# Modulation steps called from the output projection, the second GEMM's first operands loaded ahead of the residual, and stacked keys and queries turned by fp32r products

## The chip, the cores and the metric

The kernel runs on one core of a Trainium2 chip. The metric is the device time of one execution in microseconds (us); lower is better. Several executions of the kernel before were timed, and one more was profiled; the rows in this document come from the profiled one.

## The reference

Two transformer blocks work one after the other on one sequence of 1024 tokens of width 1024, all in float32. The first block projects the normalised tokens and runs three attentions on them: a sliding-window one, a sparse one that keeps the 256 best keys of each token by an index score, and one over 256 memory rows. Their outputs are projected, gated and summed, and the output projection adds the result to the residual:

```python
x = x + jnp.einsum("bsd,de->bse", merged, w_out[l])
h = rmsnorm(x, g_mlp[l])
hid = jnp.square(jax.nn.relu(jnp.einsum("bsd,df->bsf", h, w_mlp_in[l])))
x = x + jnp.einsum("bsf,fd->bsd", hid, w_mlp_out[l])
```

The second block mixes tokens by a gated recurrent scan in two directions and by pooling, and has an MLP of the same sizes (1024 to 4096 to 1024). Its norms are shifted and scaled by a modulation vector, which depends on a conditioning vector `c` alone and on nothing of the sequence:

```python
c_act = jax.nn.silu(c)
mod = c_act @ w_ada[l] + b_ada[l]          # 1024 -> 6144
sh1, sc1, gt1, sh2, sc2, gt2 = jnp.split(mod, 6, axis=-1)
```

## The kernel before, in words

Every large matrix product is made of three fp32r products: each operand is split into a rounded high part and a low remainder, and high times high, high times low and low times high are summed in PSUM. For a weight tile, ScalarE writes the high part (`wh`) and VectorE or GpSimd the low part (`wl`), in `wunit` and `parts_of`.

The order of work on each engine and each DMA queue is fixed when the program is built: a planner walks the program, gives each instruction a start by its own costs, and takes what is ready and stands earliest in the program. So an instruction may be issued well ahead of its place in the source, as soon as its data and its memory are free, but each engine and queue runs its own list strictly in order. A tile waits only for the last users of the memory that it takes over.

The stages that matter here, in order of time:

- *Attention.* `stack_q` and `stack_k` put the high and low parts of a 128-token tile of queries or keys side by side; `turn_q` and `turn_k` turn these stacks by TensorE transposes against `ident` (lines 349 and 371), four per tile of queries and two per head of keys. Between them, `fill` puts gate products (`gates_ahead`, lines 267 to 269) whose tiles stand in the pool `fwp`, the first above the weight pool on the right side of SBUF.
- *Gated sum.* For each of eight column tiles the sparse attention's projection and gate are added and split (lines 974 to 977).
- *Output projection*, `out_proj`: two halves of the tokens, eight steps of 24 products each. Before each step it calls `pre` (for the first block `x_cols`, which transposes a 128-column slice of the residual); after it, `upd` adds the product to the residual and `Stat.add` sums squares. When a half is done, its statistics give the row scale (`Stat.cols`, `spread`), and `post_out` builds the MLP's operand: `make_h` for the first half of the tokens, `make_t` for the second.
- *MLP*, `mlp`, called once for each block. Each of its two GEMMs is cut into 2 by 2 blocks with seven instead of eight block products (sums and differences of operands). The first GEMM has 16 steps `m`; the sums of weight tiles (`sums`, lines 1284 to 1287) are GpSimd's, the outputs q12, t1, t2, q21, t3, q22 and t4 are stored to DRAM (`ml_...`). The second GEMM takes four chunks `ch`; `second` loads one stored operand and splits it (ScalarE the high part, VectorE and GpSimd the low part, lines 1370 and 1371), `quarter` loads a quarter of weights, GpSimd makes sums and differences of the quarters (lines 1432, 1450, 1451, 1454), and `upd` adds each product into the residual, which is loaded back from DRAM (line 1356) into the tiles that held the first GEMM's intermediate results.
- *Modulation*, `ada`: a generator with 12 groups of 512 columns. Each group takes eight loads of 256 KB of `w_ada` into a ring of two tiles `adaw` (line 1197, SP's DMA queue), and for each load one VectorE step (line 1199 for the first, 1201 for the others). Then four TensorE transposes (line 1207) and a VectorE reduction give four columns of `mod`. `tick` advances it by one load. Before, the first block's MLP calls it: four times in each step `m` of the first GEMM and three times at each `tick2` of the second. Its pool `modp` stands where the output projection's operands (`m_hi`, `m_lo`) were.

All loads named so far go through SP's queue, most stores through ScalarE's. `begin` in `mlp` holds the pieces of the last statistics and of `make_t` that are left from the projection; `rest_t` is its second half.

Of the kernel before, what the change touches and what calls it, by code (L numbers as in the profile page):

```python
# [19 lines left out]
P = 128  # L20
# [40 lines left out]
def block_kernel(ctx, tc, x, mem, positions, g_mix, w_in, b_gate, sinks, g_mem, w_mem_kv, w_proj_swa, w_proj_dsa,  # L61
# [25 lines left out]
    def raw(ap):  # L87
        return ap.bitcast(F32)
# [23 lines left out]
    def tp_bank():  # L112
        return bank("tp")
# [5 lines left out]

    ident = cst([P, P], tag="ident")  # L120
    make_identity(nc, ident)
    mhalf = cst([P, 1], tag="mhalf")
    V.memset(mhalf, -0.5)

# [20 lines left out]
    def col(name, i):  # L145
        r0, _ = ROWS[name]
        return cols[:, r0 + i:r0 + i + 1]
# [6 lines left out]
    def h_tiles(pool):  # L154
        return tuple(pool([P, DC, 512], F32R, tag=f"h_{n}") for n in ("hi", "lo"))
# [188 lines left out]
    def turn_q(pool, st, nh):  # L344

        fill(nf["q"])
        pt = tp_bank()
        for h in range(nh):
            T.transpose(pt[:, h * P:(h + 1) * P], raw(st[:, h]).rearrange("p a b -> p (a b)"), ident)
        qT = pool([P, nh, P], F32R, tag=f"qT{nh}", bufs=QTB)  # L350
        A.copy(qT, pt[:, :nh * P].rearrange("p (h q) -> p h q", h=nh))
        return qT
# [12 lines left out]
    def turn_k(sts, dst):  # L365

        for h, st in enumerate(sts):
            fill(nf["k"])
            pt = tp_bank()
            for z in range(2):  # L370
                T.transpose(pt[:, z * P:(z + 1) * P], raw(st[:, 2 * z:2 * z + 2, :]).rearrange("p a b -> p (a b)"),
                            ident)
            for z, d in enumerate(dst(h)):
                A.copy(d, pt[:, z * P:(z + 1) * P])

# [714 lines left out]
    def mlp_dram(pool):  # L1090
        d = {n: pool([P, NM, 512], tag=f"ml_{n}") for n in OUTS}
        d["x"] = pool([P, DC, S], tag="ml_x")
        return d
# [50 lines left out]
                split_to(t4[0][:, c, :], t4[1][:, c, :], b[c])  # L1144
        rest_t.append(rest)

    xT = [hB([P, DC, 512], tag=n) for n in ("h_hi", "h_lo")]
    stp = Pool("stp", side="right", n512=4)
    xtp = Pool("xtp", side="right")
    HT[:] = [h_tiles(hA), None]  # L1150
    xs = {}

    def x_cols(hf, e):

        if e == 0:
            for j in range(4):
                xs[j] = xtp([P, D], tag="xt", bufs=4)
                nc.scalar.dma_start(xs[j], x[0, (4 * hf + j) * P:(4 * hf + j + 1) * P, :])
        pt = tp_bank()
        for j in range(4):  # L1160
            T.transpose(pt[:, j * P:(j + 1) * P], xs[j][:, e * P:(e + 1) * P], ident)
        A.copy(xT[hf][:, e, :], pt)

    mlp_d = mlp_dram(drm)

    def post_out(hf, rs):
        src = xT[hf]
        (make_h if hf == 0 else make_t)(stp, HT[hf], lambda c: src[:, c, :], rs, lambda c: col("g_mlp", c))

    pend = out_proj(stp, w_out[0], lambda k, hf: (m_hi[k][:, halves(hf)], m_lo[k][:, halves(hf)]),  # L1170
                    with_x_out(mlp_d, add_to(xT)),
                    post_out, x_cols)
    xtp.close()
    mgp.close()
    hBp = Pool("hBp")
    HT[1] = h_tiles(hBp)


    mod = cst([P, 48], tag="mod")
    bada = cst([P, 48], tag="bada")  # L1180
# [1 line left out]
    def ada(modp):  # L1182
        badr = modp([48, P], tag="badr")
        nc.scalar.dma_start(badr, b_ada_2[0].rearrange("(k p) -> k p", p=P))
        pt = tp_bank()
        T.transpose(pt[:, :48], badr, ident[:48, :48])
        V.tensor_copy(bada, pt[:, :48])
        r0, _ = ROWS["c_2"]
        s_ = modp([P, 64], tag="silu")[:, :DC]
        A.activation(s_, cols[:, r0:r0 + 8], AF.Tanh, scale=0.5)  # L1190
        V.scalar_tensor_tensor(s_, s_, 1.0, cols[:, r0:r0 + 8], op0=OP.add, op1=OP.mult)
        V.tensor_scalar(s_, s_, 0.5, None, op0=OP.mult)
        for g in range(12):
            acc = modp([P, 512], tag="ada", bufs=1)
            for k in range(DC):
                w = modp([P, 512], tag="adaw", bufs=2)
                nc.sync.dma_start(w, w_ada_2[0, k * P:(k + 1) * P, halves(g)])
                if k == 0:
                    V.tensor_scalar(acc, w, s_[:, 0:1], None, op0=OP.mult)
                else:  # L1200
                    V.scalar_tensor_tensor(acc, w, s_[:, k:k + 1], acc, op0=OP.mult, op1=OP.add)
                yield
            yield
            m4 = mod[:, g * 4:(g + 1) * 4]
            pt = tp_bank()
            for j in range(4):
                T.transpose(pt[:, j * P:(j + 1) * P], acc[:, j * P:(j + 1) * P], ident)
            V.tensor_reduce(m4, pt.rearrange("p (j q) -> p j q", j=4), axis=AX.X, op=OP.add)
            V.tensor_tensor(m4, m4, bada[:, g * 4:(g + 1) * 4], op=OP.add)

    def mlp(PB, xt, d, w1, w2, scale, post, begin, middle, tick=lambda: None, gains=None, each=lambda i, e: None,
            parts=((0, 0, 512), (1, 0, 512))):
# [75 lines left out]

        first_two(0, w_of(wp, 0, "wr", 2))
        begin[0]()  # L1290
        first_two(1, w_of(wp, 2, "wr", 2), begin[1])
        first_two(2, w_of(wp, 4, "wr", 2), eng=G)
        rest_t.pop()()
        begin[2]()
# [3 lines left out]
        for m in range(NM):  # L1298
# [10 lines left out]
            product(a, half(ua, 1), TQ["t2"])  # L1309
            V.tensor_tensor(u2, a, u2, op=OP.add)  # L1310
            V.tensor_tensor(q12, p5, u2, op=OP.add)
            for _ in range(2):
                tick()
            ub = parts_of(e1s.pop(m))
            a = mm_bank()
            product(a, half(ub, 1), B22)
# [11 lines left out]
            V.tensor_tensor(q22, p5, u3, op=OP.add)  # L1328
            relu2(q22)
            save("q22", m, q22)  # L1330
            for _ in range(2):
                tick()
            a = mm_bank()
            product(a, u4, TQ["t4"])
            V.tensor_tensor(u3, a, u3, op=OP.add)
# [15 lines left out]
        tick()  # L1351


        for hf, es in ((1, range(4)), (0, range(8)), (1, range(4, 8))):
            for e in es:
                nc.sync.dma_start(xt[hf][:, e, :], d["x"][:, e, halves(hf)])
        braw = hA([P, DC, 512], F32, tag="h_lo")
        nb = [0]

# [20 lines left out]
            return t_  # L1380

        def tick2():
            for _ in range(3):
                tick()

        def gather(to, a, ch):
# [38 lines left out]
        for ch in range(4):  # L1425
# [5 lines left out]
            for c in (0, 2):  # L1431
                G.tensor_tensor(s_[:, c:c + 2], a21[:, c:c + 2], a22[:, c:c + 2], op=OP.add)  # L1432
            b = second("q12", ch)
            for e, wt in blocks(a11):
                a = mm_bank()
                product(a, wt, b)
                gather(U[e], a, ch)
                upd(1, e, a)
            a12 = quarter(ch, 1, 0)
            tick2()  # L1440
            b = second("t1", ch)
            for e, wt in blocks(s_):
                a = mm_bank()
                product(a, wt, b)
# [87 lines left out]

    def post_mlp1(hf, st):
        if hf == 0:
            for _ in ada_["it"]:
                pass
            for i, n in ((0, "g_mix_2"), (1, "g_ffn_2")):
                r0, _ = ROWS[n]
# [21 lines left out]
               lambda c: mod[:, c:c + 1])  # L1560
        yield

    ada_ = {}

    def begin1():
        stp.close()
        ada_["it"] = ada(pools["mod"])

    def middle1():
        pools["stm"] = Pool("stm", side="right", n512=2)  # L1570

    def tick1():
        next(ada_["it"], None)

    pools["mod"] = Pool("modp")
    mlp(hBp, xT, mlp_d, w_mlp_in[0], w_mlp_out[0], None, post_mlp1,
        (lambda: next(pend), lambda: next(pend), begin1), middle1, tick1, gsq)
    pools["mod"].close()
    drm.close()
    HT[:] = h2  # L1580

# [107 lines left out]
            gates_half(0)  # L1689
    gates_half(1)  # L1690
    pools["stm"].close()
    pt = tp_bank()
    for t in range(NT):
        T.transpose(pt[:, t * 16:(t + 1) * 16], zT[:, t * P:(t + 1) * P], ident[:16, :16])
# [403 lines left out]
```

## Time and profile before

| | |
|---|---|
| median of 3 runs | 2720.86 us (2717.14 to 2721.62) |
| the profiled execution | 2721.95 us, of which the span from first to last instruction is 2720.2 us |
| mean granted TensorE clock | 0.972 of full speed |
| busy share of the span | PE (matmul) 93%, PEld (weight loads) 77%, DVE (VectorE) 69%, ACT (ScalarE) 44%, POOL (GpSimd) 36% |
| DMA | 338.57 MB, 124 GB/s over the span |
| first block's output projection | about 781 to 880 us |
| first block's MLP, first GEMM's 16 steps | about 943 to 1300 us |
| second block's MLP, first GEMM's 16 steps | about 2091 to 2378 us |

Reading it: times are us from the span's start unless marked ns. A busy PE is not yet PE at its peak: at the lower of the two clocks each matmul takes longer and counts as busy all the same. "A <- B" in a row of waits means that A's engine sat idle until B was done; the numbers after it are the us in total, how many times, and the longest. `SPq`, `ACTq` are DMA queues' own instructions. The engine names are those of the table.

### The profile page before, as it was taken

How to read it: one execution, taken by the hardware profiler on the slowest of the kernel's cores; microseconds unless marked ns; L12 is line 12 of the kernel's file. 1: busy time of each engine (PE TensorE's matmuls, PEld its weight loads, DVE VectorE, ACT ScalarE, POOL GpSimd, SP SyncE). 2: the span in 40 equal slices, each digit the busy share in tenths (PEclk: the TensorE clock that was granted, in tenths of full speed). 3: DMA queues.
4: the chain of work that ended last, by engine and by line, in shares of the span. 5: the costliest groups of instructions: out<-in, count | busy, mean ns of one | idle time of the engine just before them, and what ended most of it. 6: DMA issues, size and time to landing. Idle time of an engine off the chain costs nothing. (4 is left out here: it accounts for less than half of the span.)

```text
span 2720.2 us, 34915 instructions
## 1 busy us (share of the span) xinstructions
PE 2528.9 (93%) x12560; PEld 2107.4 (77%) x12560; DVE 1882.7 (69%) x3206; ACT 1197.9 (44%) x2218; POOL 988.1 (36%) x717
## 2 busy tenths in 40 slices
PE   7999999899999678888899979999997999989997
PEld 6899987788878566667688856888786788768886
DVE  7685878834455866676778896755658565578898
ACT  6575765335334433334433333323335554543433
POOL 3011123421002533333755661211334443476554
PEclk9999999999999889999999989999998999999999
DMA  3121022321155266666644301422343444753431
GB/s 114 53 61 40 25 79 90 89 61 41 63 183 179 78 203 200 202 204 230 220 170 155 109 24 51 156 63 70 120 152 97 160 150 159 250 204 134 170 109 62
DMA packets 275712, 338.57 MB, mean 124 GB/s; under 512 B 14268, under 2 KB 185044, under 8 KB 268372
## 3 DMA queue, kind: packets, MB, share of 16 engines
q1 hardware_dynamic: 234820, 253.65, 29.2%
q10 hardware_dynamic: 40720, 82.70, 8.3%
q8 instruction: 99, 1.62, 0.2%
q14 instruction: 73, 0.60, 0.1%
HBM read 250.25 MB, written 86.05 MB: 124 GB/s over the span
## 5 line engine op out<-in xcount | busy, mean ns | idle before, releaser
L1233 PE MATMUL mm<-h_hi,wh 128*128 128x512 f32 (+1 forms) x1136 | 455.5, 401 | 33.3 <-ACT wh L1227 17.2
L1235 PE MATMUL mm<-h_hi,wl 128*128 128x512 f32 (+1 forms) x1136 | 452.1, 398 | 10.5 <-DVE wl L1228 10.5
L1234 PE MATMUL mm<-h_lo,wh 128*128 128x512 f32 (+1 forms) x816 | 322.2, 395 | 0.0
L1233 PEld LDWEIGHTS mm<-h_hi,wh 128*128 128x128 f32 x1136 | 221.4, 195 | 82.2 <-ACT wh L1227 20.6
L1235 PEld LDWEIGHTS mm<-h_hi,wl 128*128 128x128 f32 x1136 | 220.7, 194 | 63.4 <-DVE wl L1228 18.2
L1227 ACT CAST wh<-q 128x1024 fp32r<-128x1024 f32 x116 | 121.7, 1052 | 331.7 <-PE mm L1234 297.7
L1234 PE MATMUL mm<-h_hi,wh 128*128 128x512 f32 (+1 forms) x624 | 244.8, 392 | 13.2 <-POOL h_hi L1371 13.2
L1228 DVE TENSOR_TENSOR wl<-q,wh 128x1024 fp32r<-128x1024 f32 x116 | 162.9, 1405 | 32.9 <-ACT wh L1227 31.3
L1234 PEld LDWEIGHTS mm<-h_lo,wh 128*128 128x128 f32 x816 | 158.3, 194 | 31.6
L1371 POOL TENSOR_TENSOR h_hi<-h_lo,h_hi 128x512 fp32r<-128x512 f32 x76 | 128.6, 1712 | 113.1 <-ACT h_hi L1370 107.9
L133 ACT CAST wh<-wr 128x1024 fp32r<-128x1024 f32 (+5 forms) x107 | 97.2, 911 | 149.7 <-PE mm L418 43.5
L1233 PE MATMUL mm<-q,wh 128*128 128x512 f32 x384 | 151.3, 394 | 10.4 <-DVE q L1119 10.4
L1235 PE MATMUL mm<-q,wl 128*128 128x512 f32 x384 | 150.2, 392 | 8.0 <-DVE wl L1228 8.0
L1234 PE MATMUL mm<-q,wh 128*128 128x512 f32 x384 | 150.9, 393 | 0.0
L1234 PEld LDWEIGHTS mm<-h_hi,wh 128*128 128x128 f32 x624 | 120.5, 193 | 37.9 <-POOL h_hi L1371 14.4
L1284 POOL TENSOR_TENSOR sa<-wr 128x512 f32<-128x512 f32 x32 | 41.7, 1303 | 264.8 <-DMA wr<-in_w_ff_dram 60.5
L134 POOL TENSOR_TENSOR wl<-wr,wh 128x1024 fp32r<-128x1024 f32 (+5 forms) x40 | 78.1, 1958 | 160.7 <-ACT wh L133 159.2
L1615 PE MATMUL mm<-h_hi,wh 128*128 128x512 f32 x320 | 132.0, 412 | 0.8 <-DVE kn L1648 0.8
L1617 PE MATMUL mm<-h_hi,wl 128*128 128x512 f32 x320 | 126.7, 396 | 0.0
L1371 DVE TENSOR_TENSOR h_hi<-h_lo,h_hi 128x512 fp32r<-128x512 f32 x76 | 120.4, 1605 | 8.3 <-ACT h_hi L1370 8.3
L1616 PE MATMUL mm<-h_lo,wh 128*128 128x512 f32 x320 | 125.5, 392 | 0.0
L1233 PE MATMUL mm<-h_lo,wh 128*128 128x512 f32 (+1 forms) x304 | 115.4, 380 | 0.6 <-ACT wh L1227 0.6
(589 smaller groups left out, 7006.9 us busy)
## 6 DMA issues: line engine op xcount, KB each, us to landing
h_lo<-ml_t SPq DMA_DIRECT2D x32, 1024.0 KB
adaw<-in_w_ada_dram SPq DMA_DIRECT2D x96, 256.0 KB
h_lo<-ml_q SPq DMA_DIRECT2D x24, 1024.0 KB
wr<-in_w_in_dram SPq DMA_DIRECT2D x42, 512.0 KB
wr<-in_w_out_dram SPq DMA_DIRECT2D x32, 512.0 KB
ml_t<-h_lo ACTq DMA_DIRECT2D x64, 256.0 KB
q<-in_w_mlp_out_dram SPq DMA_DIRECT2D x16, 1024.0 KB
ml_t<-x ACTq DMA_DIRECT2D x64, 256.0 KB
```

The source lines that it names most:

```text
L133: A.copy(hi, r)
L134: (eng or V).tensor_tensor(lo, r, raw(hi), op=OP.subtract)
L1227: A.copy(hi, r)
L1228: (eng or V).tensor_tensor(lo, r, raw(hi), op=OP.subtract)
L1233: mm(a, wt[0][:, k], b[0][:, k, sl], start=(k == 0), stop=False)
L1234: mm(a, wt[0][:, k], b[1][:, k, sl], start=False, stop=False)
L1235: mm(a, wt[1][:, k], b[0][:, k, sl], start=False, stop=(k == 3))
L1284: G.tensor_tensor(sa[:, 0:4], e2[:, 0:4], e2[:, 4:8], op=OP.add)
L1371: (G if c % 2 else V).tensor_tensor(lo[:, c], r[:, c], raw(hi[:, c]), op=OP.subtract)
L1615: mm(a, hi[:, k, :], r_hi, start=(k == 0), stop=False)
L1616: mm(a, hi[:, k, :], r_lo, start=False, stop=False)
L1617: mm(a, lo[:, k, :], r_hi, start=False, stop=(k == DC - 1))
```

## The change

```diff
+    identR = cst([P, P], F32R, tag="identR")
+    V.tensor_copy(identR, ident)
...
     # turn_q
-            T.transpose(pt[:, h * P:(h + 1) * P], raw(st[:, h]).rearrange("p a b -> p (a b)"), ident)
+            mm(pt[:, h * P:(h + 1) * P], st[:, h].rearrange("p a b -> p (a b)"), identR, start=True, stop=True)
     # turn_k
-                T.transpose(pt[:, z * P:(z + 1) * P], raw(st[:, 2 * z:2 * z + 2, :]).rearrange("p a b -> p (a b)"),
-                            ident)
+                mm(pt[:, z * P:(z + 1) * P], st[:, 2 * z:2 * z + 2, :].rearrange("p a b -> p (a b)"), identR,
+                   start=True, stop=True)
...
     # ada (now defined ahead of the output projection)
-                nc.sync.dma_start(w, w_ada_2[0, k * P:(k + 1) * P, halves(g)])
+                nc.gpsimd.dma_start(w, w_ada_2[0, k * P:(k + 1) * P, halves(g)])
...
-            yield
+            for _ in range(3):
+                yield
             m4 = mod[:, g * 4:(g + 1) * 4]
...
+    modp = Pool("modp", side="right")
+    ada_ = ada(modp)
+    def tick1(n=1):
+        for _ in range(n):
+            next(ada_, None)
...
     # x_cols
         A.copy(xT[hf][:, e, :], pt)
+        tick1(4)
...
     # mlp, ahead of the first GEMM's steps
-        first_two(1, w_of(wp, 2, "wr", 2), begin[1])
+        first_two(1, w_of(wp, 2, "wr", 2))
+        begin[1]()
...
     # mlp, first GEMM, at both places of step m
-            for _ in range(2):
-                tick()
+            tick()
...
     # mlp, second GEMM
-        for hf, es in ((1, range(4)), (0, range(8)), (1, range(4, 8))):
-            for e in es:
-                nc.sync.dma_start(xt[hf][:, e, :], d["x"][:, e, halves(hf)])
+        def x_back():
+            for hf, e0 in ((0, 0), (0, 4), (1, 0), (1, 4)):
+                nc.sync.dma_start(xt[hf][:, e0:e0 + 4, :], d["x"][:, e0:e0 + 4, halves(hf)])
...
         def tick2():
-            for _ in range(3):
+            for _ in range(2):
                 tick()
...
             b = second("q12", ch)
+            if not ch:
+                bt = second("t1", ch)
+                x_back()
             for e, wt in blocks(a11):
                 a = mm_bank()
                 product(a, wt, b)
                 gather(U[e], a, ch)
-                upd(1, e, a)
+                upd(1, e, a if ch else U[e])
             a12 = quarter(ch, 1, 0)
             tick2()
-            b = second("t1", ch)
+            b = second("t1", ch) if ch else bt
...
-    pools["mod"] = Pool("modp")
     mlp(hBp, xT, mlp_d, w_mlp_in[0], w_mlp_out[0], None, post_mlp1,
         (lambda: next(pend), lambda: next(pend), begin1), middle1, tick1, gsq)
-    pools["mod"].close()
...
     # second block, after its gates
     pools["stm"].close()
+    modp.close()
```

So the modulation's generator starts ahead of the output projection, in a pool on the right side of SBUF that stays open until the second block's gates; its loads are issued by GpSimd; four of its steps stand in each of the 16 projection steps, two in each step `m`, two at each `tick2`, and three instead of one step lie between a group's last load and its transposes. The changes in `mlp` hold for both blocks; only the first block passes it a `tick`.

## Rows read from the trace of the kernel before

**Rows 1.** The page's part 1: busy us (share of the span) xinstructions of each engine.

```profile
PE 2528.9 (93%) x12560; PEld 2107.4 (77%) x12560; DVE 1882.7 (69%) x3206; ACT 1197.9 (44%) x2218; POOL 988.1 (36%) x717
```

**Rows 2.** Windows: stretch, length, PE, PEld, DVE, ACT, POOL busy (xcount), PEclk, DMA share, GB/s.

```profile
716.00:781.00 65.00, 65.00 (x286) 53.37 (x287) 30.75 (x51) 20.83 (x33) 0.00 (x0) 1.00 0.45 140
781.00:880.00 99.00, 97.49 (x461) 79.09 (x460) 50.49 (x61) 39.60 (x59) 17.35 (x13) 1.00 0.58 184
880.00:943.00 63.00, 41.00 (x163) 32.02 (x162) 54.08 (x69) 26.94 (x45) 30.95 (x20) 0.81 0.27 84
943.00:1300.00 357.00, 305.26 (x1260) 240.64 (x1259) 245.69 (x316) 141.49 (x213) 129.21 (x91) 0.94 0.63 209
...
2091.00:2378.00 287.00, 281.41 (x1230) 231.37 (x1229) 160.73 (x199) 145.55 (x213) 125.69 (x91) 0.99 0.53 177
```

**Rows 3.** The tile adaw: op xcount, ns min/median/max, first and last start; who waited.

```profile
L1197 SPq DMA_DIRECT2D adaw<-in_w_ada_dram x96: 327/328/1405, 880.0 to 1227.2; - x96
L1201 DVE SCALAR_TENSOR_TENSOR ada<-adaw,silu,ada x84: 732/752/1803, 888.0 to 1232.2; 128x512 f32<-128x512 f32 x84
L1199 DVE TENSOR_SCALAR ada<-adaw,silu x12: 473/600/1469, 886.5 to 1214.4; 128x512 f32<-128x512 f32 x12
...
  DVE ada L1201: 61.4, 36
```

**Rows 4.** Waits of SP's queue, 945 to 1300 us: us, times, longest.

```profile
SPq L1197 <- DVE ada L1201: 65.4, 73, 2.6
SPq L1197 <- DMA adaw<-in_w_ada_dram: 52.4, 34, 4.0
SPq L1197 <- DVE ada L1199: 39.2, 8, 6.2
```

**Rows 5.** Waits of PE: whole span, and 880 to 945 us.

```profile
PE tp L1207 <- DVE ada L1201: 26.4, 9, 12.2
...
PE tp L1035 <- POOL st_r L127: 10.2, 1, 10.2
```

**Rows 6.** Line 267, the gate filler's products: first and last start.

```profile
L267 PE MATMUL fl<-h_hi,fh x160: 387/396/628, 101.8 to 714.2; 128*128 128x512 f32 x160
```

**Rows 7.** DMA issues between 945 and 1300 us.

```profile
adaw<-in_w_ada_dram SPq DMA_DIRECT2D x87, 256.0 KB
```

**Rows 8.** Timeline of DVE: start, us, engine, line, op, tiles [idle before].

```profile
1097.65 0.75 DVE L1201 SCALAR_TENSOR_TENSOR ada<-adaw,silu,ada 128x512 f32<-128x512 f32 x1 [2.89 <-DMA adaw<-in_w_ada_dram]
1100.85 0.75 DVE L1201 SCALAR_TENSOR_TENSOR ada<-adaw,silu,ada 128x512 f32<-128x512 f32 x1 [2.45 <-DMA adaw<-in_w_ada_dram]
...
1105.88 0.75 DVE L1201 SCALAR_TENSOR_TENSOR ada<-adaw,silu,ada 128x512 f32<-128x512 f32 x1 [0.79 <-DMA adaw<-in_w_ada_dram]
```

**Rows 9.** Waits of PE, 1250 to 1350 us and 2350 to 2420 us.

```profile
PE mm L1234 <- POOL h_hi L1371: 7.4, 1, 7.4
PE mm L1233 <- ACT wh L1227: 6.0, 1, 6.0
...
PE mm L1234 <- POOL h_hi L1371: 5.8, 1, 5.8
PE mm L1233 <- ACT wh L1227: 3.6, 2, 1.8
```

**Rows 10.** Timeline of POOL.

```profile
1311.29 6.07 POOL L1451 TENSOR_TENSOR q<-q,q 128x1024 f32<-128x1024 f32 x2
```

**Rows 11.** Timeline of PE: queries' transposes, and fp32r products 128 columns wide.

```profile
675.25 0.64 PE L349 MATMUL tp<-ident,stq 128*128 128x128 f32 x4
675.65 0.48 PE L385 MATMUL sc<-kd_hi,qT 128*128 128x512 f32 x1
675.97 0.39 PE L386 MATMUL sc<-kd_lo,qT 128*128 128x512 f32 x1
...
225.69 0.28 PE L386 MATMUL sc<-ks_lo,qT 128*128 128x128 f32 x1
225.80 0.27 PE L385 MATMUL sc<-ks_hi,qT 128*128 128x128 f32 x1
```

More of the change, by code (lines that the diff above doesn't have):

```diff
@@ L1145, in make_t @@
         rest_t.append(rest)
[L1147 to L1176, printed above, removed]
     mod = cst([P, 48], tag="mod")
@@ L1209, in ada, with x_cols, post_out @@
             V.tensor_tensor(m4, m4, bada[:, g * 4:(g + 1) * 4], op=OP.add)
+    modp = Pool("modp", side="right")
[3 more added lines that the diff above has]
+            next(ada_, None)
+    xT = [hB([P, DC, 512], tag=n) for n in ("h_hi", "h_lo")]
+    stp = Pool("stp", side="right", n512=4)
+    xtp = Pool("xtp", side="right")
+    HT[:] = [h_tiles(hA), None]
+    xs = {}
+    def x_cols(hf, e):
+        if e == 0:
+            for j in range(4):
+                xs[j] = xtp([P, D], tag="xt", bufs=4)
+                nc.scalar.dma_start(xs[j], x[0, (4 * hf + j) * P:(4 * hf + j + 1) * P, :])
+        pt = tp_bank()
+        for j in range(4):
+            T.transpose(pt[:, j * P:(j + 1) * P], xs[j][:, e * P:(e + 1) * P], ident)
+        A.copy(xT[hf][:, e, :], pt)
+        tick1(4)
+    mlp_d = mlp_dram(drm)
+    def post_out(hf, rs):
+        src = xT[hf]
+        (make_h if hf == 0 else make_t)(stp, HT[hf], lambda c: src[:, c, :], rs, lambda c: col("g_mlp", c))
+    pend = out_proj(stp, w_out[0], lambda k, hf: (m_hi[k][:, halves(hf)], m_lo[k][:, halves(hf)]),
+                    with_x_out(mlp_d, add_to(xT)),
+                    post_out, x_cols)
+    xtp.close()
+    mgp.close()
+    hBp = Pool("hBp")
+    HT[1] = h_tiles(hBp)
     def mlp(PB, xt, d, w1, w2, scale, post, begin, middle, tick=lambda: None, gains=None, each=lambda i, e: None,
@@ L1330, in mlp @@
             save("q22", m, q22)
-            for _ in range(2):
-                tick()
+            tick()
             a = mm_bank()
@@ L1534, in post_mlp1 @@
         if hf == 0:
-            for _ in ada_["it"]:
+            for _ in ada_:
                 pass
@@ L1561, in h2_half @@
         yield
-    ada_ = {}
     def begin1():
         stp.close()
-        ada_["it"] = ada(pools["mod"])
     def middle1():
         pools["stm"] = Pool("stm", side="right", n512=2)
-    def tick1():
-        next(ada_["it"], None)
-    pools["mod"] = Pool("modp")
     mlp(hBp, xT, mlp_d, w_mlp_in[0], w_mlp_out[0], None, post_mlp1,
         (lambda: next(pend), lambda: next(pend), begin1), middle1, tick1, gsq)
-    pools["mod"].close()
     drm.close()
```

## The prediction

> **What bounds the kernel now.** I read the page's shares first: TensorE is busy for 93% of the span [rows 1], so time can be won only where it idles or runs at the lower clock. Then the windows [rows 2]: in the output projection (781 to 880 us) TensorE is busy 97.5 of 99 us, but in the first GEMM's 16 steps of the first block's MLP only 305.3 of 357 us, at a mean granted clock of 0.94. The second block runs the same 16 steps in 287 us, 281.4 busy, at 0.99. The steps' own work is the same, so the first block's MLP pays 70 us for something that the second has not: 46.1 us of idle time (51.7 against 5.6) and 23.9 us of products at the lower clock, which came after idle stretches. The one thing that the first has alongside is the modulation.
>
> The tile adaw shows how [rows 3]: its 96 loads run from 880.0 to 1227.2 us, one in 3.65 us (347.2/95), far ahead of their places in the program, the last of which lie in the second GEMM; so the planner pulls them forward to where their memory becomes free, the end of the output projection. VectorE waits 61.4 us for them, 0.64 us for each of 96. SP's queue, which also brings the MLP's weights, stands still 157 us (65.4 + 52.4 + 39.2) for the ring of two tiles [rows 4]. And TensorE waits 26.4 us at the groups' transposes [rows 5]. Elsewhere two more places idle: the row scale at the projection's end (10.2 us [rows 5]) and the start of both second GEMMs [rows 9].
>
> **The change part by part**, made against the profiled execution's 2721.95 us (span 2720.2 and 1.75 around it; the median of the runs is 1.1 below).
>
> *Modulation, first GEMM.* The pool now stands where the gate filler's tiles were, whose last products start at 714.2 us [rows 6], so the loads can begin at about 716 instead of 880. At 3.65 us each, 164/3.65 = 45 are done by 880; the stretch to 943 took 9 before (96 less the 87 of [rows 7]) and I leave it so; 42 remain for the 16 steps instead of 87. I let the excess of 70 us follow the number of loads: it falls to 70 x 42/87 = 34, a gain of 36. The two added yields put the transposes later in the list: of their 26.4 us some 11.6 (42/96) would be left, and I take half as gone, 6. Together -42. Bounds: all 70 if no load reaches the steps, 10 if each of those left costs almost twice as much, because GpSimd's queue, which issues the loads now, also makes the weight sums that the step needs next.
>
> *Modulation, output projection and the stretch before it.* What is moved there must fit on VectorE, since SP's queue is no longer touched and GpSimd is busy only 17 of 99 us. A load costs 0.75 us of VectorE [rows 8] and 0.64 of waiting. From 716 to 781 us VectorE has 30.75 us of 65; 18 loads add 25: covered. From 781 to 880 it has 50.5 of 99; 27 loads add 38, which fits (88). If all 48 loads that the 64 called steps hold fall there, it is 50.5 + 67 = 117, 18 us too many. The splits of the weights stand behind a waiting load on VectorE, and the products wait for them, but weights are split up to three tiles ahead, some 18 us. I take +6, nearer the end that the measured rate gives; bounds 0 and +18. Loads from GpSimd's queue appear in no row here; the nearest are SP's. The Trainium skill, "DMA: Bandwidth & Descriptors", section "Anatomy of one DMA — SWDGE (gpsimd) path", has about 2.0 us fixed plus the bytes at 436 GB/s for one, so 2.6 us for 256 KB as an estimate; with the step's 0.75 us that is 3.35 us where the ring never runs ahead, 48 loads take 161 us instead of 99, and by it the sum would come to 2661 + 62 - 6 = 2717.
>
> *The projection's end.* TensorE waits 10.2 us for the row scale [rows 5], which VectorE reaches after the first modulation steps (line 1199 first starts at 886.5 and 1201 at 888.0 [rows 3]). The generator's start is over by then, but its loads go on: -5, bounds -10 and 0. The piece of `make_t` that now follows the whole of `first_two(1)` is fed by VectorE, busy 54 of 63 us here [rows 2]; no work leaves that chain, and TensorE's 12 products (12 x 0.227 = 2.7 us; 0.227 is 65 us for 286 products in [rows 2]) now stand ahead of the transposes that start it: +1 for both blocks, bounds 0 and +3, as in the second block the wait at this place is short already.
>
> *Second GEMM's start.* Two waits stand there in both blocks [rows 9]. ScalarE's high part of the first weights waits for a load that SP's queue issues behind the residual's (6.0 and 3.6 us); the residual's tiles are the last that the first GEMM frees. And the low part of t1 waits on GpSimd behind the sums for t2 and q21 (7.4 and 5.8 us): line 1451 holds GpSimd 6.07 us [rows 10], line 1450 stands before it, and neither is needed so early. With t1 split ahead of the products and the residual loaded after both operands, both waits lose their cause: 22.8 us. What is late next: the residual, now 4 MB in four loads, at 317 GB/s (184 at a DMA share of 0.58 [rows 2]) 13 us, while the four q12 products take 48 x 0.227 = 10.9; so about 3 us come back. -20; bounds -4 (the residual holds VectorE and with it the next weights) and -30 (the slower clock that follows such waits goes too).
>
> *Turns by fp32r products.* Four transposes take 0.40 us (675.25 to 675.65), and the next product 0.32 instead of 0.23 [rows 11]; fp32r products of 128 columns come every 0.11 us (225.69 to 225.80), four in 0.44. So between -0.05 and +0.04 us for each of 38 tiles of queries (6, 8, 16 and 8 by the loops), and about nothing for the keys' pairs: -1, bounds -2 and +2. The added copy of the identity is one short VectorE instruction at the start, beside the first loads.
>
> Sum: -42 + 6 - 5 + 1 - 20 - 1 = -61, so 2661 in the profile's terms, 2660 as a median. The favourable ends add up to -112 (2610), the unfavourable to -10 + 18 + 0 + 3 - 4 + 2 = +9 (2731).
>
> **The rivals.**
>
> 1. *VectorE becomes the projection's bound* (slower). Four steps stand in each projection step of 6 us, and the ring has two tiles: if a load's cycle is C and the planner leaves the steps where the program has them, 48 loads need 48 C from 781 us on, and the groups' transposes hold TensorE's list to it. It decides from 48 C - 99 > 66, C = 3.4 us. One cycle of 3.2 us stands in [rows 8] (1097.65 to 1100.85); with GpSimd's issue at 4.0 us it is +93 - 42 - 5 - 20 = +26: 2747. Against it: five loads in the same rows, from 1097.65 to 1105.88, come every 2.06 us, and the planner has run ahead wherever memory allowed. The Trainium skill, "SBUF — State Buffer", section "Who interferes with whom", speaks for it: a DVE instruction in a two-port mode locks GpSimd out, and with it the descriptors of a load that GpSimd issues. No row here shows a load held up so; line 1199's least 473 ns against 1201's 732 [rows 3] makes it the likeliest to do it, at one load in eight.
>
> 2. *The loss only changes queues.* The weight sums wait on GpSimd behind the loads as SP's loads did before: the first GEMM gains 10 instead of 42. -10 + 6 - 5 + 1 - 20 - 1 = -29: 2692. For it: two steps in each m still carry a load, and the ring still has two tiles. Against: the product that frees a tile then lies some 9 us back.
>
> 3. *The residual takes the place of the waits removed.* VectorE's additions for q12 stand ahead of the splits for t1's weights and wait for the residual's second half: 0 instead of -20, so -41: 2680.
>
> 4. *All loads are through before the 16 steps.* At the 2.06 us above, 96 loads take 198 us, 716 to 914. The first GEMM comes to its twin's 287: -70; the denser steps cost the projection 10, the row scale gains nothing: -70 + 10 + 0 + 1 - 20 - 1 = -80: 2641.
>
> **How the numbers follow.** Forecast 0.38, rival 4 0.18, rival 2 0.17, rival 3 0.16, rival 1 0.11. The range goes from 2612, the favourable ends, to 2716, above rivals 2 and 3 with some of rival 1's milder cases; most of rival 1 lies outside. A change of 0.2% (5.4 us) is about what can be told from none here. Only rival 1 reaches it on the slow side (0.11); no change needs rival 2 with little gain at the second GEMM (0.03); faster is the rest, 0.86.
>
> **What would show it.** Right: loads of w_ada begin near 716 us and about 40 of them fall into the 16 steps; these take some 315 us instead of 357; waits at line 1207 halve; POOL h_hi and ACT wh are gone at both second GEMMs' starts; the projection stays within 6 us of its 99. Wrong: an output projection above 130 us with TensorE waiting for line 1207 or for `wl` (rival 1); waits of POOL sa (line 1284) and of `wl` in the steps as long as before (rival 2); TensorE waiting at the second GEMM's start for `wl` behind line 1377 (rival 3); no load after 943 us (rival 4). The prediction fails as a whole if the first GEMM's excess was not the loads', so that it stays with them gone.

## The result and the profile after

The changed kernel takes 2747.52 us (median; 2745.63 to 2748.68) against 2721.24 for the kernel before (2717.14 to 2725.24): ratio 1.0095, 95% interval 1.0081 to 1.0108, some 26 us slower. The forecast was 2660, the range 2612 to 2716. The profiled execution has a span of 2743.9 us, 23.7 more than before.

I read the stages first, from the first and last instruction of each in the two traces. Changes of length in us: attention +7.4 (the last gate filler product starts at 721.6 us instead of 714.2 [rows 6]), gated sum +5.3 (67.4 to 72.7), output projection +27.9 (97.7 to 125.6), from there to the first store of the first GEMM +3.0 (64.4 to 67.4), its 16 steps, up to the last `ml_q` store, -25.4 (355.1 to 329.7), start of the second GEMM, from there to the first copy into `v`, -0.7 in block 1 and +2.9 in block 2. From there to block 2's first `ml_q` store it is +5.0, in block 2's 16 steps -4.1, and between the last output's DMA and the end +2.9 (4.5 to 7.5).

One of these borders moves with the change. The last `ml_q` store of block 1 is issued 5.8 us after the second GEMM's first product in the kernel before, 3.1 us after it in the changed one; up to that product the 16 steps are 22.7 us shorter, not 25.4. The windows after (columns as in [rows 2]):

```profile
716.00:794.00 78.00, 74.34 (x339) 60.80 (x338) 38.80 (x65) 23.00 (x38) 4.83 (x9) 0.98 0.48 147
794.00:920.00 126.00, 102.89 (x478) 82.53 (x477) 81.99 (x109) 40.49 (x58) 38.03 (x49) 0.95 0.70 214
920.00:987.00 67.00, 42.33 (x171) 33.15 (x170) 54.14 (x68) 26.88 (x45) 32.70 (x27) 0.80 0.27 81
987.00:1317.00 330.00, 293.40 (x1222) 235.10 (x1221) 203.71 (x259) 145.12 (x214) 152.16 (x134) 0.94 0.55 184
2114.00:2395.00 281.00, 275.49 (x1206) 226.26 (x1205) 162.14 (x200) 144.94 (x214) 126.52 (x91) 1.00 0.51 171
```

The first and third lines are the stretches ahead of and behind the projection. The first is 13 us longer, because it also holds the 7.4 us by which attention ends later; the stages themselves are 5 and 3 us longer. In the projection (second line) TensorE idles 23 us where it idled 1.5 [rows 2], at a granted clock of 0.95 instead of 1.00. The 16 steps gained, but are still 49 us above their twin in block 2 (last line). The tile adaw, as in [rows 3], with what its loads waited for on GpSimd:

```profile
L1168 POOL DMA_DIRECT2D adaw<-in_w_ada_dram x96: 536/538/780, 699.9 to 1136.3; - x96
L1172 DVE SCALAR_TENSOR_TENSOR ada<-adaw,silu,ada x84: 734/751/6876, 730.6 to 1139.3; 128x512 f32<-128x512 f32 x84
...
  DVE ada L1172: 100.5, 60
...
  DVE ada L1172: 87.4, 54
  PE tp L1179: 25.8, 5
...
DMA to landing us min/median/max: 2.8/3.5/7.1
```

A load now costs GpSimd 0.54 us of its own time, and GpSimd waits 100.5 us for VectorE's steps (third line); VectorE's steps wait 87.4 us for the loads (fourth) where it was 61.4. TensorE's waits for the groups' transposes have not shrunk: 25.8 us are put down to VectorE's steps, where it was 26.4. Of these 13.4 are in the projection (first line below). The 6.4 of the second line, put down to ScalarE, come on top; they are the same kind of wait, for the step that the transposes need ends at 833.67 us, 0.15 before they start. So 19.8 us stand in the projection:

```profile
PE tp L1179 <- DVE ada L1172: 13.4, 3, 8.9
PE tp L1179 <- ACT t L1003: 6.4, 1, 6.4
PE tp L1037 <- POOL st_r L129: 2.5, 1, 2.5
```

What VectorE and GpSimd do before those last transposes, in their timelines (columns as in [rows 8]):

```profile
828.11 0.75 DVE L1172 SCALAR_TENSOR_TENSOR ada<-adaw,silu,ada 128x512 f32<-128x512 f32 x1 [0.70 <-DMA adaw<-in_w_ada_dram]
831.66 0.75 DVE L1172 SCALAR_TENSOR_TENSOR ada<-adaw,silu,ada 128x512 f32<-128x512 f32 x1 [2.80 <-DMA adaw<-in_w_ada_dram]
832.33 0.68 DVE L1066 TENSOR_TENSOR h_hi<-mm,h_hi 128x512 f32<-128x512 f32 x1
832.93 0.74 DVE L1172 SCALAR_TENSOR_TENSOR ada<-adaw,silu,ada 128x512 f32<-128x512 f32 x1
833.59 1.22 DVE L136 TENSOR_TENSOR wl<-wr,wh 128x1024 fp32r<-128x1024 f32 x1
```
```profile
827.70 0.55 POOL L1168 DMA_DIRECT2D adaw<-in_w_ada_dram  x1 [0.84 <-DVE ada L1172]
829.16 0.54 POOL L1168 DMA_DIRECT2D adaw<-in_w_ada_dram  x1 [0.91 <-DVE ada L1172]
832.71 0.54 POOL L1168 DMA_DIRECT2D adaw<-in_w_ada_dram  x1 [3.01 <-DVE ada L1172]
```

A step ends at 828.86, the load that takes its tile is issued 0.30 us later, and each of the two tiles in turn makes VectorE wait; the addition for the projection and the split `wl` stand behind, and TensorE stands at the transposes until 833.8.

### The profile page after: what moved, and what is told of

It reads as the page before. It is cut to its first block, busy times and chain, and to the rows that moved or that the text cites. A ratio compares the mean times of both kernels' runs of the same rounds, so it can differ in the third digit from the quotient of the medians.

```text
span 2743.9 us, 34962 instructions
## 1 busy us (share of the span) xinstructions
PE 2537.7 (92%) x12560; PEld 2117.5 (77%) x12560; DVE 1892.3 (69%) x3207; ACT 1199.2 (44%) x2218; POOL 1041.8 (38%) x813
## 3 DMA queue, kind: packets, MB, share of 16 engines
q1 hardware_dynamic: 220612, 228.48, 25.8%
## 5 line engine op out<-in xcount | busy, mean ns | idle before, releaser
L1245 PE MATMUL mm<-h_lo,wh 128*128 128x512 f32 (+1 forms) x816 | 321.1, 393 | 0.0
L1246 PEld LDWEIGHTS mm<-h_hi,wl 128*128 128x128 f32 x1136 | 219.1, 193 | 62.8 <-DVE wl L1239 18.5
L1239 DVE TENSOR_TENSOR wl<-q,wh 128x1024 fp32r<-128x1024 f32 x116 | 175.2, 1512 | 31.7 <-ACT wh L1238 30.4
L1245 PEld LDWEIGHTS mm<-h_hi,wh 128*128 128x128 f32 x624 | 120.2, 193 | 23.9
L1172 DVE SCALAR_TENSOR_TENSOR ada<-adaw,silu,ada 128x512 f32<-128x512 f32 x84 | 76.9, 915 | 87.8 <-DMA adaw<-in_w_ada_dram 87.4
L1239 DVE TENSOR_TENSOR wl<-we,wh 128x1024 fp32r<-128x1024 f32 x56 | 88.1, 1574 | 52.2 <-ACT wh L1238 52.2
L1168 POOL DMA_DIRECT2D adaw<-in_w_ada_dram x96 | 52.3, 545 | 186.4 <-DVE ada L1172 100.5
```

The lines of the kernel that those rows point to most:

```text
L1239: (eng or V).tensor_tensor(lo, r, raw(hi), op=OP.subtract)
L1245: mm(a, wt[0][:, k], b[1][:, k, sl], start=False, stop=False)
L1246: mm(a, wt[1][:, k], b[0][:, k, sl], start=False, stop=(k == 3))
```

## The experiments

Each ratio is to the kernel before, timed on the same chip. Line numbers in some kernels are shifted by a few. Stage lengths from the traces, as above (us; loads counted by the start of their steps on VectorE; the waits are VectorE's idle time before the 96 steps):

| kernel | gated sum | projection (loads in it) | to first store | 16 steps (loads) | waits for loads |
|---|---|---|---|---|---|
| before | 67.4 | 97.7 (0) | 64.4 | 355.1 (89) | 62.1 |
| changed | 72.7 | 125.6 (36) | 67.4 | 329.7 (45) | 91.7 |
| e2 modulation alone | 72.2 | 129.1 (36) | 68.3 | 333.1 (45) | 92.5 |
| e6 the same, SP's queue | 69.8 | 118.0 (35) | 61.7 | 317.2 (45) | 57.9 |
| e7 the same, two loads in all | 67.4 | 105.4 (-) | 62.4 | 304.0 (-) | 5.6 |
| e8 two steps for four | 72.9 | 102.9 (16) | 69.1 | 358.3 (67) | 97.0 |
| e9 old place, GpSimd | 67.4 | 97.7 (0) | 64.1 | 383.8 (89) | 98.7 |
| e5 no modulation | 67.4 | 98.0 (-) | 63.1 | 284.9 (-) | - |
| e13 as e2, four tiles in the projection | 67.5 | 119.2 (46) | 59.8 | 330.5 (45) | 55.1 |
| e14 as e13, SP's queue | 67.4 | 117.0 (46) | 62.2 | 317.2 (45) | 44.6 |

**Which part costs what** (e1 to e4, each alone on the kernel before). e1 has the diff's lines of `identR`, `turn_q` and `turn_k`; e2 those of `ada`, `modp`, `tick1` and the ticks; e3 those of `x_back`, `bt` and `upd(1, e, a if ch else U[e])`; e4 this:

```diff
-        first_two(1, w_of(wp, 2, "wr", 2), begin[1])
+        first_two(1, w_of(wp, 2, "wr", 2))
+        begin[1]()
```

> The kernel before with the turns of the stacks alone. Theory from the two traces (attention ends 7.4 us later in the changed kernel): the turns cost, time +5 to +8 us, and the last gate filler product ends about 7 us later than in the kernel before. Rival, the prediction's term: -2 to +2 us, and the 7.4 us come from somewhere else.

Measured 1.0031 (1.0020 to 1.0042), +8.4 us: the turns cost. The last filler product starts 6.5 us later and the later stages differ by 1 us or less. The queries' stacks, before and in e1 (columns as in [rows 3]):

```profile
L349 PEld LDWEIGHTS tp<-ident,stq x152: 137/140/144, 41.4 to 675.5; 128*128 128x128 f32 x152
```
```profile
L351 PEld LDWEIGHTS tp<-identR,stq x152: 186/190/192, 40.8 to 682.0; 128*128 128x128 f32 x152
```

The stack is the operand that is loaded as weights in either form, and as fp32r its load takes 190 ns instead of 140. With 232 turns (152 and 80 for the keys) that would be up to 11.6 us where nothing covers it; 6.5 show. That these loads are the cause is not shown: from 30 us to the last filler product TensorE is only 2.5 us busier (664.4 to 666.9), the rest is idle time, and the order of its list has changed too (the turns stand in 41 and 47 runs instead of 40 and 50).

> The kernel before with the modulation's part alone (pool and generator ahead of the projection, loads issued by GpSimd, four steps in each projection step, fewer ticks in the MLP, three yields). Theory from the two traces: gated sum +5, projection +28, first GEMM -25, end of the program +3: together +8 to +15 us, and the projection takes 125 us instead of 99. Rival, the prediction's terms: -41 us, the slow projection comes from the other parts.

Measured 1.0068 (1.0054 to 1.0083), +18.5 us; projection 129.1. More than the theory's upper end, but its sign and places hold; the prediction's -41 is out.

> The kernel before with the second GEMM's start alone (t1's operand and then the residual behind q12's operand, the first additions from the copy). Theory from the two traces (block 1 -0.7, block 2 +2.9 between the last store of the first GEMM and the first of the second's v): -3 to +4 us. Rival, the prediction's term: -20 us, and in the changed kernel something of the modulation hides it.

Measured 0.9970 (0.9959 to 0.9982), -8.2 us: between the two. Counted by TensorE's own block products (twelve instructions each), from the start of the MLP's 109th (the first GEMM has 112) to that of its 129th, the second GEMM's start takes 74.8 us in block 1 and 71.0 in block 2 in the kernel before, 69.9 and 69.3 in e3, and 67.5 and 71.0 in the changed kernel. So 6.6 us of e3's gain lie where they were expected. TensorE's waits there in e3, 1293 to 1360 us, to be read beside the first two lines of [rows 9]:

```profile
PE mm L1235 <- DVE wl L1228: 4.6, 2, 2.6
PE mm L1233 <- ACT wh L1227: 3.3, 1, 3.3
```

> The kernel before with the piece of make_t behind the whole of first_two(1) alone. Theory and prediction agree: 0 to +3 us, the stretch between projection and first steps 0 to 2 us longer in each block. Rival: the +3.0 us of the changed kernel there are the modulation's, then 0 here.

Measured 0.9996 (0.9986 to 1.0006): nothing that can be told from no change. The four parts sum to +18 where the whole is +26; the difference is about their joint uncertainty, and whether the parts disturb each other is left open.

**Was the premise right?** e5 is the kernel before with the groups cut down to the bias, so that their loads, steps and transposes are left out:

```diff
         for g in range(12):
-            acc = modp([P, 512], tag="ada", bufs=1)
...
+            m4 = mod[:, g * 4:(g + 1) * 4]
+            V.tensor_copy(m4, bada[:, g * 4:(g + 1) * 4])
+            yield
```

> The kernel before without the modulation's work: no loads of w_ada, no steps, no transposes; mod is the bias alone. Theory, the prediction's first step: the 70 us by which the first block's 16 steps exceed the second's are the modulation's, so these take 285 to 295 us instead of 357 and the time falls by 60 to 80 us. Rival: the excess is the first block's own (a lower clock, GpSimd's sums), the steps stay above 320 us and the time falls by less than 40.

Measured 0.9738 (0.9724 to 0.9753), 2651.93 us, -71. The 16 steps in e5's windows:

```profile
942.00:1227.00 285.00, 277.30 (x1207) 227.86 (x1206) 160.55 (x197) 144.52 (x211) 122.84 (x90) 0.99 0.53 179
```

The excess of 70 us was the modulation's, idle time and lower clock alike. So the question is why moving half of it did not move half of its price.

**The queue, the steps' number, the loads** (e6 to e8 on e2, e9 on the kernel before):

```diff
# e6 (and e16 on the changed kernel); e9 the other way round on the kernel before
-                nc.gpsimd.dma_start(w, w_ada_2[0, k * P:(k + 1) * P, halves(g)])
+                nc.sync.dma_start(w, w_ada_2[0, k * P:(k + 1) * P, halves(g)])
# e7: ws are two tiles, loaded once; all 96 steps stay
-                w = modp([P, 512], tag="adaw", bufs=2)
-                nc.gpsimd.dma_start(w, w_ada_2[0, k * P:(k + 1) * P, halves(g)])
+                w = ws[k % 2]
# e8
-        tick1(4)
+        tick1(2)
...
             V.tensor_tensor(q12, p5, u2, op=OP.add)
             tick()
+            tick()
```

> The modulation part alone, its loads issued on SP's queue again instead of by GpSimd. Theory: a ring of two tiles makes each load wait for the step two before it, whatever queue issues it, so the projection stays at 115 to 130 us, and the weights on SP's queue stand behind waiting loads besides: within 10 us of the modulation part alone (2742), rather slower. Rival: GpSimd's issue makes the loads late; then the projection falls to 105 us or less and the time by 15 us or more.

Measured 0.9939 (0.9922 to 0.9955), 2704.60 us: 38 us less than e2 by the medians, 35 by the ratios, and faster than the kernel before. My theory was wrong. The projection is only 11 us shorter, but the 16 steps are too, by 16.

> The modulation part alone, with two loads in all: the 96 steps take the first two tiles over and over, all steps, transposes and reductions stay. Theory, the loads' cycle is what holds the projection: 98 to 106 us instead of 129, hardly a wait of TensorE at the groups' transposes, time 2690 or less. Rival, VectorE's own work of 64 steps is too much beside the projection: 115 us or more.

Measured 0.9835 (0.9820 to 0.9850), 2678.64 us; projection 105.4, as the theory had it. VectorE's own work is the smaller part. Side by side, e7, e6 and e2 split the price roughly: of the projection's 31 us over the kernel before, 8 are the steps by themselves, 13 the loads on SP's queue and 11 GpSimd's queue; of the 48 us of the 16 steps over e5, 19, 13 and 16.

> The modulation part alone with two steps instead of four in each projection step, and one more in the first half of each step m. Theory: two loads in 6.2 us are within the cycle of a ring of two, the projection takes 99 to 106 us, and the first GEMM gives back part of its gain (333 to 345 us): time 2715 to 2730. Rival: the planner runs ahead to where memory allows whatever the program says, the projection stays above 120 us and the time within 5 us of 2742.

Measured 1.0077 (1.0062 to 1.0092), 2744.15 us. Neither: the projection came down to 102.9 as the theory said, and the steps went up to 358.3, so the time stayed at e2's. The 20 loads taken out of the projection made it 26 us shorter, and the 22 more in the steps made these 25 us longer.

> The kernel before, the modulation where it was, its loads issued by GpSimd: the fourth corner beside the kernel before (old place, SP: 2722), the modulation part alone (new place, GpSimd: 2742) and the same with SP (new place: 2705). Theory: the queue costs some 38 us wherever the steps stand, so about 2750 to 2765. Rival: GpSimd's issue is bad only in the new place, where its loads stand in its list behind the statistics; then 2715 to 2730.

Measured 1.0109 (1.0094 to 1.0124), 2753.41 us, +28: the queue costs in the old place as well, so it is not the new place's list. What it does there, waits between 945 and 1330 us in e9 (the last store of the 16 steps is at 1325.8):

```profile
PE mm L1235 <- DVE wl L1228: 44.7, 26, 5.0
PE mm L1233 <- ACT wh L1227: 19.4, 12, 2.9
...
PE tp L1207 <- DVE ada L1201: 1.4, 2, 0.8
```
```profile
DVE ada L1201 <- DMA adaw<-in_w_ada_dram: 91.1, 64, 4.1
```

The same stretch in the kernel before:

```profile
PE mm L1235 <- DVE wl L1228: 15.8, 17, 1.9
```

The transposes' 26.4 us [rows 5] are gone, but TensorE waits 44.7 us instead of 15.8 for splits (`wl`) that stand on VectorE behind steps that wait for loads. In the new place it is alike: 16.4 us for `wl` in the 16 steps of e2, 7.0 in e6. Taking each load with the step for which it was issued, in all 96 pairs: SP's queue issues into a tile 0.03 us after the step that read it ended (median), GpSimd 0.30 us, and its issue takes 0.54 us. From the start of the issue to the step, where the step waited, there is no such difference (medians, e6 4.12 us, e2 3.86). So what differs is how late the load is issued.

The medians hide a second part of it. GpSimd has work of its own in the same list, the weight sums and the statistics, and a load whose tile is free stands behind that work: in e2 18 of the 94 loads that take a tile over are issued 0.9 to 6.3 us after its release, in e6 two. The longest, on GpSimd and then on VectorE:

```profile
985.38 2.28 POOL L1328 TENSOR_TENSOR h_lo<-h_hi,h_lo 128x512 f32<-128x512 f32 x1
987.60 1.09 POOL L1166 DMA_DIRECT2D adaw<-in_w_ada_dram  x2
```
```profile
992.37 0.75 DVE L1170 SCALAR_TENSOR_TENSOR ada<-adaw,silu,ada 128x512 f32<-128x512 f32 x1 [5.27 <-DMA adaw<-in_w_ada_dram]
```

The step that freed the tile had ended at 981.32 us. The steps of these 18 loads wait 13.5 of e2's 92.5 us. VectorE's waits for loads are 35 us longer with GpSimd's queue in the new place and 37 in the old (last column: e2 and e6, e9 and before), the time 35 to 38 and 28 us.

**Is it the ring of two?** On e2, e13 (GpSimd's queue) and e14 (SP's) give the ring two tiles more, from the pool that is open only in the projection:

```diff
-                w = modp([P, 512], tag="adaw", bufs=2)
+                nl[0] += 1
+                more = extra and nl[0] % 4 >= 2
+                w = extra[0]([P, 512], tag="adawx", bufs=2) if more else modp([P, 512], tag="adaw", bufs=2)
...
     xtp = Pool("xtp", side="right")
+    extra.append(xtp)
```

> The modulation part alone (loads issued by GpSimd), with a ring of four tiles instead of two inside the output projection. Theory, the cycle of a ring of two: the projection falls from 129 to 112 us or less, VectorE's waits for loads there from 34 to under 15, time 2720 to 2730. Rival, the order of the lists and the statistics in GpSimd's: the projection stays at 120 us or more, time within 8 us of 2742.

Measured 0.9992 (0.9982 to 1.0002), 2719.41 us, 23 us less than e2 (21 by the ratios). VectorE's waits for loads in the projection, e2 (784 to 913 us) and then e13 (782 to 901):

```profile
DVE ada L1170 <- DMA adaw<-in_w_ada_dram: 32.1, 20, 2.9
DVE ada L1168 <- DMA adaw<-in_w_ada_dram: 1.7, 2, 0.9
```
```profile
DVE ada L1172 <- DMA adawx<-in_w_ada_dram: 6.3, 6, 2.7
DVE ada L1172 <- DMA adaw<-in_w_ada_dram: 1.6, 1, 1.6
```

They are 7.9 us instead of 33.8: the ring's cycle was what made the loads late. The projection fell to 119.2 only, between the two expectations, but it now holds 46 loads instead of 36. The two further tiles exist only from the projection on (the first load into one is issued at 782.4 us), so two loads instead of eight come before it. That is why the gated sum is back at 67.5, 5 us less than e2; the way to the first store is 59.8, 8 us less.

> The same with the loads on SP's queue. Theory: the projection falls from 118 to 109 us or less, VectorE's waits for loads there from 15 to about 5; time 2692 to 2698 for 2705. Rival: the loads come no faster, because other loads and stores stand ahead on SP's queue; projection 115 us or more, time within 5 us of 2705.

Measured 0.9927 (0.9912 to 0.9942), 2701.74 us; projection 117.0: the rival. VectorE's steps there wait 13.6 us for their loads, 15.9 in e6. With SP's queue a longer ring moves the time little, though the projection holds 46 loads instead of 35. Beside e13 this shows what the queue needs to cost so much: with four tiles GpSimd's queue costs the projection 2 us (119.2 and 117.0), with two 11 (129.1 and 118.0), and in the 16 steps, where the ring has two tiles in all four kernels, 13 and 16. Some 117 us is left with either queue, against 105 without the loads (e7). In e14 TensorE waits there for a bank behind VectorE once (5.5 us), for the transposes (3.6) and for the residual's loads (2.5), at a DMA share of 0.77 and a clock of 0.96; which of the loads' effects is the first cause I have not separated.

**The second GEMM.** e11 is e3 with the first additions from PSUM:

```diff
-                upd(1, e, a if ch else U[e])
+                upd(1, e, a)
```

> The second GEMM's start alone, but the first additions to the residual take the product from PSUM as before, not from its copy in SBUF. Theory: the copy costs VectorE 2.06 us for one instead of 0.68, because GpSimd works on SBUF beside it; four of them in each block are 5.5 us that VectorE is late with the next weights; 4 to 10 us less than with the copy (2715): 2705 to 2711. Rival: the products hold their banks until the residual is back, TensorE waits for a bank instead: 2715 or more.

Measured 0.9956 (0.9941 to 0.9971), 2712.43 us: some 4 us below e3's 0.9970, but the intervals overlap. Counted by products as above, the second GEMM's start takes 67.6 and 66.8 us, 4.8 us less than e3 in the two blocks together. The term itself is plain in the groups of VectorE's instructions between 1295 and 1345 us, e3 and then e11 (count, busy us, mean ns):

```profile
L1377 DVE TENSOR_TENSOR h_lo<-u,h_lo 128x512 f32<-128x512 f32 x4 | 8.0, 2058 | 0.0
L1371 DVE TENSOR_TENSOR h_hi<-h_lo,h_hi 128x512 fp32r<-128x512 f32 x4 | 2.6, 678 | 0.0
```
```profile
L1377 DVE TENSOR_TENSOR h_lo<-mm,h_lo 128x512 f32<-128x512 f32 x4 | 2.5, 678 | 0.0
```

The second line is a subtraction that also has two SBUF operands. It takes 0.68 us as well, because these four run after 1328.9 us, while GpSimd rests: here two operands in SBUF cost more only beside GpSimd.

**Put together.** e10 is the changed kernel without the turns and with SP's queue; e12 is e10 with e11's line; e15 is e12 with the ring of four; e16 is the changed kernel with SP's queue.

> The whole change without the fp32r turns and with the modulation's loads on SP's queue. Theory, the parts add up: 2705 for the modulation with SP, 8 less for the second GEMM's start, 1 less for the piece of make_t: 2693 to 2700, ratio 0.988 to 0.992. Rival: the residual's and t1's loads, now on one queue with the modulation's, take the gain of the second GEMM back: 2703 or more.

Measured 0.9925 (0.9908 to 0.9941), 2702.40 us: just above the theory's 0.992 and at the rival's edge; the parts add up to within some 5 us (0.9939, 0.9970 and 0.9996 make 0.9905), which the intervals do not tell from nothing.

> As the kernel with the change without turns and with SP's queue, and the first additions from PSUM. Theory: less than that kernel by the same 4 to 10 us, about 2690. Rival: no less, or more.

Measured 0.9909 (0.9889 to 0.9929), 2698.47 us: 4 us below e10, with overlapping intervals again.

> The kernel without turns, with SP's queue and the first additions from PSUM (0.991 of before), with the ring of four in the projection besides. Theory: 8 to 12 us less than without the ring, ratio 0.986 to 0.989. Rival: the ring moves nothing, 0.990 to 0.992.

Measured 0.9905 (0.9890 to 0.9919), 2695.96 us: the rival; the ring adds nothing that can be told here. e12 and e15 beat both kernels, by 0.9% the one before and by 1.8% the changed one (0.9909/1.0095).

> The changed kernel with one word put back: the modulation's loads on SP's queue. Theory: the queue's 38 us go and the turns' 8 stay, 2705 to 2714, ratio 0.994 to 0.997, so faster than the kernel before. Rival: in the whole change the loss of the projection has another root beside the queue, 2725 or more.

Measured 0.9952 (0.9936 to 0.9969), 2708.55 us: with that one word put back, the changed kernel is faster than the one before, by 13 us, and 39 us faster than it was; projection 117.8, 16 steps 315.5.

## Why the prediction was wrong

The step that put the time outside the range is the price of a load. "Loads from GpSimd's queue appear in no row here; the nearest are SP's": the terms were summed with SP's numbers, and the queue alone is 39 us (2747.52 to 2708.55 in e16, which lies inside the range). Two terms were out of their bounds with SP's queue as well, the output projection and the turns. Term by term:

- *First GEMM, -42.* The premise held (e5), though the 23.9 us that I put down to the lower clock also hold up to 8.6 us of the groups' own 48 transposes. So did the count: 45 loads are left in the 16 steps, 42 were forecast. By the projection's end 44 are done, 45 were forecast. With SP's queue the gain follows too: 355.1 to 317.2 us in e6 and 315.5 in e16, -38 and -40, of which some 2.5 in e16 are the moved border. In the changed kernel it is -25, in e2 -22: within the bounds, but little more than half. The step that failed is "I let the excess of 70 us follow the number of loads", with a price per load taken from SP's queue: over the 284.9 us of e5, a load in the steps costs 0.79 us in the kernel before (70.2/89), 0.72 in e6 (32.3/45), but 1.07 with GpSimd's queue (48.2/45 in e2) and 1.11 in the old place (98.9/89, e9). The waits at the transposes did not shrink as forecast: 25.8 us in the changed kernel and 23.1 in e6, from 26.4.
- *Output projection, +6 (0 to +18).* Measured +27.9, +31.4 in e2, +20.3 in e6: out of bounds with either queue. The failed step is that 27 loads add 38 us to VectorE, "which fits (88)": it counted busy time, 0.75 us and 0.64 of waiting for each load, while the list is strictly in order and the groups' transposes hold TensorE to it (19.8 us in the changed kernel, 8.1 in e6). And the loads came later than forecast: 8 instead of 18 before the projection, because the second group needs the one tile `ada`, which the first group's transposes free only at 812.6 us (801.1 in e6), at their place in TensorE's list; 36 instead of 27 fell into the projection. The stretch before it, forecast as covered, lost 5.3 us (2.4 in e6); there it is the waiting and not the steps, for with the same eight steps and no loads the gated sum keeps its 67.4 (e7).
- *Projection's end, -5.* +3.0 in the changed kernel, -2.7 in e6, -4.9 in e16: the size came out with SP's queue, the reason did not. With no modulation at all (e5) TensorE still waits 8.6 us for the row scale, 10.2 before, so the modulation's first steps account for some 1.6 us of that wait. What shortened the stretch in e16 is open.
- *begin[1], +1.* e4: -1 with an interval from -4 to +2.
- *Second GEMM's start, -20.* -8 in e3. Of the two waits POOL h_hi is not there any more in either block, but ACT wh has only fallen, from 6.0 to 3.3 us in block 1 and from 3.6 to 2.9 in block 2, and waits for `wl` stand in their place (4.6 us in block 1). The failed step is that both waits "lose their cause", with only the residual late next. What was late next was VectorE. The additions from the copy take 2.06 us each instead of 0.68, and the splits of the weights 2.2 us instead of 1.5 in the mean between 1295 and 1345 us, while GpSimd works on its sums beside them. This is what the Trainium skill, "SBUF — State Buffer", section "Who interferes with whom", has: a VectorE instruction with two SBUF inputs contends with a GpSimd instruction that reads SBUF; one with a single SBUF input, outside the two-port modes, does not. The trace agrees, 2.06 us against 0.68. The prediction drew on that section for the loads, and not for the one operand that the diff moves from PSUM to SBUF. Taking that operand from PSUM again gives some 4 us back (e11), and the waits that are left stand at the weights, whose high part comes late from ScalarE and whose split is slow. How the rest of the missing 12 shares out was not separated.
- *Turns, -1 (-2 to +2).* +8.4. The bounds came from products that follow each other at 0.11 us in a stream of their own kind; that such a stream says what a few turns between other products cost was the step that failed. The load of the stack as weights, 190 ns for 140, was in no row that I took, though the trace of before had both kinds; whether it is the 8.4 us is open (e1).
- *The program's end, +2.9:* not foreseen; it is there in each kernel in which GpSimd issues all of these loads (the end comes 7.2 to 7.5 us after the last output's DMA, 4.5 to 5.2 in the others).

Rival 1, slower at 2747, came out in the time by luck and in the mechanism by half. The ring's cycle decides, as e13 shows, but the cycle is 2.9 us per load (5.75 for a tile, median in e2), below the 3.4 us from which it was to decide and the 4.0 with which it was priced, and the projection lost 28 us and not 93; the price met the result because the first GEMM then gained 25 and not 42 and two parts cost that were priced at gains. The estimate from the Trainium skill, "DMA: Bandwidth & Descriptors", section "Anatomy of one DMA — SWDGE (gpsimd) path", 2.6 us for 256 KB, is near the 2.9 us (median) from the end of the issue to landing in the changed kernel. The release and the issue ahead of it, 0.30 and 0.54 us, come on top.

## What to carry to other kernels

A step moved to an engine with free time is free only if its data is there when its turn comes; in a short ring count the whole cycle of a tile (step, release, issue, landing), and the queue that issues is part of it: one word was 35 to 39 us. Ask too what else the issuing engine has in its list, for a load stands behind that. Where work is spread over stages, its price moves with it (e8), so compare prices per piece at both places before moving. When an operand goes from PSUM to SBUF, look at what GpSimd does beside it.

## What the runs showed of the hardware

A 256 KB load issued by GpSimd holds that engine for 0.54 us and is issued 0.30 us after its tile is released, against 0.03 us on SP's queue (medians), and later where GpSimd's own work stands ahead, up to 6.3 us in e2; the time from issue to use is alike (3.86 and 4.12 us). A 128x128 stack is loaded as TensorE weights in 190 ns as fp32r and in 140 as the fp32 operand of a transpose. An addition of two SBUF operands of 128x512 took 2.06 us beside GpSimd's additions, 0.68 with one operand in PSUM; a subtraction of two SBUF operands of that size took 0.68 while GpSimd rested.
